# Layer 1 of a two-layer diffusion trunk: where norm 2's scale and bias are applied to its residual, and where 24 products of its modulation are computed

## The chip, the cores and the metric

The kernel runs on 1 core of one Trainium2 chip. The metric is the device time of one execution in microseconds. The engines are PE (TensorE, matrix products, with PEld for its weight loads), DVE (VectorE), ACT (ScalarE), POOL (GpSimd) and SP (SyncE, which issues nearly all the DMAs here).

## The reference, cut to what matters

Two post-norm layers over 1024 latent tokens and 256 context tokens of width 1024, all in float32. Four token mixers run side by side on one modulated stream, and a SwiGLU feed-forward follows:

```python
for l in range(2):
    m  = split(silu(c)     @ w_mod[l] + b_mod[l], 6)     # six rows of 1024
    mc = split(silu(c_ctx) @ w_mod[l] + b_mod[l], 6)
    h, hc = x * (1 + m[1]) + m[0], ctx * (1 + mc[1]) + mc[0]
    y = concat(mixers(h @ w_in[l], hc @ w_in[l])) @ w_out[l]
    x = layer_norm(alpha * x + m[2] * y, ln1_g[l], ln1_b[l])
    x = layer_norm(alpha * x + m[5] * swiglu(x * (1 + m[4]) + m[3]), ln2_g[l], ln2_b[l])
    # the same two lines for ctx with mc, in layer 0 alone
```

The change is about two things in it: the `ln2_g[0], ln2_b[0]` of the `x` that enters `alpha * x + m[2] * y` in layer 1, and the rows `m[2]`, `m[3]`, `m[4]` of layer 1.

## The kernel before, in words

**Tiles.** Tokens are cut into tiles of 128 (0 to 7 latent, 8 and 9 context). A tile of 128x1024 float32 fills one of 47 slots in SBUF that serve nearly everything. Matrix products are made from float32 operands in two parts, a high part (`hi`, cast on ACT) and the rest (`lo`, a subtraction on DVE), with three products for each pair (`split`, `mm3`). Instructions are kept in order on each engine; the order is found when the kernel is built, from the program's order and from what is expected to be ready.

**Stages.** Each layer has an in-projection (`inproj`), attention, an out-projection (`outproj`), the feed-forward's first half (`ffn_up`) and its second half (`ffn_down`, in layer 0 with `ffn_ctx` before it). In layer 1 the in-projection works through ten "c tiles" (416 columns), eight "d tiles" (512 columns, gated by a 128x128 mix) and ten "f units" (128 rows of output each).

**Modulation.** A row of `m` is made of eight products: a 128x1024 piece of `w_mod` is loaded (`mod_load`) and multiplied and summed against the broadcast `silu(c)` on DVE (`mod_tile`, L244). `silu_rows` loads that row and puts it through ACT.

**Background.** `self.bg` is a list of small steps. `background()` takes one off the list: after each tile of the in-projection, and four times in each pass of `ffn_up` over a pair of hidden blocks (19 such passes a layer, once, twice and once at three places of the pass).

**Before the change.** Layer 0's `ffn_up` has 24 modulation pieces in its background (its own row 5, layer 1's rows 1 and 0), each in two steps, a load and a product, and then 10 tiles of norm 1's scale and bias (`start`, `fetch`, `affine`). Layer 1's in-projection has 8 empty steps and then the 24 pieces of its rows 2, 4 and 3.

**The residual.** `norm2(0)` stores the normalised rows of layer 0 without scale and bias in `zd[1]`. In layer 1's `outproj`, `prepare(t)` loads such a tile (`resid_in`), multiplies it by `ln2_g` and adds `ln2_b` on POOL (`affine_row`, L1374 and L1375), and splits the tile's attention output into `ys`, four pieces on ACT (L147) and DVE (L149). `product` multiplies by the out-projection weights (L1329). `finish` gates the result (L1338), adds the residual (L1339), normalises (`stats` on DVE, `rstd` on POOL, L162 and L163, `nb` on DVE, L182) and, some tiles later, transposes pairs of tiles for the feed-forward (`to_stream`, L1255 to L1268). Tiles 0 and 1 and the last two are multiplied as pairs, the others alone; `prepare` runs one tile ahead, and at the last single tile two. Layer 0's `outproj` is the same without `affine_row`, and over ten tiles.

Of the kernel before, what the change touches and what calls it, by code (L numbers as in the profile page):

```python
# [14 lines left out]
ALU = mybir.AluOpType  # L15
# [15 lines left out]
PAUSE = 8  # L31
# [57 lines left out]
class Kern:  # L89
# [454 lines left out]
    def inproj(self, l):  # L544
        nc, a, ws = self.nc, self.a, self.ws
        last = l == DEPTH - 1
        self.cT = [self.slot(F32, "cT") for _ in range(4)]
        self.cTx = self.slot(F32, "cTx")
        base = 0 if l == 0 else self.w_in1
        def n1(t):  # L550
            return 160 if last and t >= 8 else 416
        rows = self.slot(F32, "drow")
        self.drow = rows
        self.y = [[None, None] for _ in range(4)]

        def late():
            t0 = self.slot(F32, "dws")
            nc.sync.dma_start(out=t0[:, :512], in_=a["dws"][l])
            dh, dl = self.slot(R, "dws"), self.slot(R, "dws")
            self.dws = (dh[:, :512], dl[:, :512])  # L560
            self.split(t0[:, :512], *self.dws)
            self.y[3] = [self.slot(F32, "y") for _ in range(2)]
            self.yx = [None, self.slot(F32, "yx") if not last else None]

        def load_drow():
            nc.sync.dma_start(out=rows[:, :512], in_=a["dln"][l].partition_broadcast(128))

        def load_krt():
            self.krt = self.tmp()
            nc.sync.dma_start(out=self.krt, in_=a["krt"])  # L570

        def c_tiles(units, tiles):
            self.cw = 416
            self.chunk(l, units, n1, tiles, lambda t, ps: self.post_c(l, t, ps, n1(t)))

        def d_tiles(units, tiles):
            self.cw = 512
            self.chunk(l, units, lambda t: 512, tiles, lambda t, ps: self.post_d(l, t, ps))

        def four(i):  # L580
            return [ws.get(base + i + j) for j in range(4)]

        if l == 0:
            ps, dots = self.first_stream()
            load_drow()
            load_krt()
            self.late_constants()
            late()
            units = four(4)
            for t in range(8):  # L590
                for i in POSTS.get(t, ()):
                    self.post_d(l, i, ps[i], 1)
                if t == CTX_AT:
                    for f in dots:
                        f()
                    self.first_ctx()
                c_tiles(units, [t])
            base += 4
            c_tiles(units, [8])
            ws.split_to(base + 4 + C_EARLY)  # L600
            c_tiles(units, [9])
            units = four(4)
            ws.split_to(base + 8 + F_EARLY)
            self.queue_mod(0, (2, 4, 3), (0, 1))
            d_tiles(units, (8, 9))
        else:
            self.silu_rows(("c",))
            self.queue_mod(1, (2, 4, 3), (0,), PAUSE)
            load_drow()
            load_krt()  # L610
            units = four(0)
            ws.load_to(base + 6)
            c_tiles(units, (8, 9) + tuple(range(8)))
            units = four(4)
            late()
            ws.load_to(base + 9)
            d_tiles(units, range(8))

        self.rope = [self.slot(F32, "rope") for _ in range(2)]
        for i in range(2):  # L620
            nc.sync.dma_start(out=self.rope[i], in_=a["ropeA"][i])
        self.fA = [None] * 4
        self.fB = [None] * 6
        self.fAx = self.slot(F32, "fAx")
        self.fBx = [self.slot(F32, "fBx") for _ in range(2)]
        for f in range(10):
            wh, wl = ws.get(base + 8 + f)
            ws.split_to(min(base + 10 + f, base + 18))
            ws.load_to(base + 11 + f)
            dst = self.slot(F32, "f")  # L630
            isq = f in (0, 1, 4, 5)
            for g in range(2 if last and isq else 3):
                n = 512 if g < 2 else 256
                ps = self.p1("f")
                for kt in range(8):
                    w0 = 128 * kt
                    self.mm3(
                        ps[:, :n], wh[:, w0:w0 + 128], wl[:, w0:w0 + 128], self.hT(0, kt, 512 * g, n),
                        self.hT(1, kt, 512 * g, n), kt == 0, kt == 7,
                    )  # L640
                self.tick()
                self.post_f(f, g, ps, dst)
                self.background(BG_IN)
            if f < 4:
                self.fA[f] = dst
            else:
                self.fB[f - 4] = dst
        self.flush()
        while self.bg:
            self.background()  # L650
# [636 lines left out]
    def outproj(self, l):  # L1287
        nc, a, ws = self.nc, self.a, self.ws
        last = l == DEPTH - 1
        nt = 8 if last else 10  # L1290
# [3 lines left out]
            self.affine_cols(self.sb_ff[l][c], l, c, 3, 4, self.cols[:, l, 0:8], self.cols[:, l, 8:16])  # L1294
        W = {}
        row = self.gate_row(l, 0, 2)
        if l:
            pg, pb = self.load_row(a["ln2g"][l - 1]), self.load_row(a["ln2b"][l - 1])
        self.g = [[None] * 3 for _ in range(2)]
        xs, ys, ps, zs = {}, {}, {}, []  # L1300

        def prepare(t):
            if t >= nt:
                return
            xs[t] = self.resid_in(l, t)
            if l:
                self.affine_row(xs[t], pg, pb)
            yh, yl = ys[t] = self.slot(R, "ys"), self.slot(R, "ys")
            if t < 8:
                parts = [(256 * q, 256, self.y[q][t // 4], 512, 128 * (t % 4)) for q in (3, 0, 1, 2)]  # L1310
            else:
                parts = [(512 * q, 512, self.yx[q], 256, 128 * (t - 8)) for q in (0, 1)]
            for o, n, y, w, c in parts:
                v = lambda s: s[:, o:o + n].rearrange("p (k c) -> p k c", c=128)
                self.split(y.rearrange("p (k c) -> p k c", c=w)[:, :, c:c + 128], v(yh), v(yl))
# [41 lines left out]
        for g in groups:  # L1357
# [11 lines left out]
                    ws.split_to(self.w_ff[l] + min(i // 2, 2))  # L1369
            for t in g:  # L1370
                finish(t)

    def affine_row(self, x, g, b):
        self.nc.gpsimd.tensor_tensor(out=x, in0=x, in1=g, op=ALU.mult)  # L1374
        self.nc.gpsimd.tensor_tensor(out=x, in0=x, in1=b, op=ALU.add)  # L1375


    def ffn(self, l):
# [156 lines left out]
    def ffn_up(self, l):  # L1535


        nc, ws = self.nc, self.ws
# [36 lines left out]
        for j in range(PLAIN, NHID):  # L1575
# [22 lines left out]
            self.mm12(B, W["S3"], hs["T3"], True)  # L1598
            h1 = self.tmp()
            nc.vector.tensor_tensor(out=h1, in0=A, in1=e, op=ALU.add)  # L1600
            self.background(2)
            self.mm12(X, W["g2"], hs["21"], False)
            nc.vector.tensor_tensor(out=h1, in0=B, in1=h1, op=ALU.add)
            if not last:
# [3 lines left out]
                self.mm12(pg, W["g1"], hs["x1"], True, 256)  # L1608
                self.mm12(pg, W["g2"], hs["x2"], False, 256)
            prep[3]()  # L1610
            self.mm12(A, W["S4"], hs["22"], False)
            s0 = self.tmp()
            nc.scalar.activation(out=s0, in_=X, func=AF.Silu)  # L1613
# [30 lines left out]
    def up_background(self, l):  # L1644

        nc, a = self.nc, self.a
        last = l == DEPTH - 1
        cs = (0,) if last else (0, 1)
        steps, held = [], {}

        def dots(ll, nt):
            self.mod_tile(ll, nt, held.pop("w"), cs)
            if nt % 8 == 7:
                for c in cs:
                    self.mod_finish(ll, c, nt // 8)

        def load(ll, nt):
            held["w"] = self.mod_load(ll, nt)

        for ll, v in [(l, 5)] + ([] if last else [(l + 1, 1), (l + 1, 0)]):  # L1660
            for nt in range(8 * v, 8 * v + 8):
                steps += [lambda ll=ll, nt=nt: load(ll, nt), lambda ll=ll, nt=nt: dots(ll, nt)]


        rows = []

        def start():
            rows.extend((self.load_row(a["ln1g"][l]), self.load_row(a["ln1b"][l])))
            for r in rows:
                nc.vector.tensor_scalar(out=r, in0=r, scalar1=ALPHA, scalar2=None, op0=ALU.mult)  # L1670

        def fetch(t):
            x = held["x"] = self.slot(F32, "x1")
            nc.sync.dma_start(out=x, in_=self.zd[0][128 * t:128 * t + 128])

        def affine(t):
            x = held.pop("x")
            nc.vector.tensor_tensor(out=x, in0=x, in1=rows[0], op=ALU.mult)
            nc.vector.tensor_tensor(out=x, in0=x, in1=rows[1], op=ALU.add)
            nc.sync.dma_start(out=self.zd[2][128 * t:128 * t + 128], in_=x)  # L1680

        steps.append(start)
        for t in range(8 if last else 10):
            steps += [lambda t=t: fetch(t), lambda t=t: affine(t)]
        self.silu_rows(("c",) if last else ("c", "cc"))
        return steps

    def down_blocks(self):
        out, j = [], 0
# [362 lines left out]
```

## Time and profile before

| | us |
|---|---|
| median of 3 runs | 3012.97 |
| lowest, highest | 3010.84, 3014.16 |
| the profiled execution | 3017.34 |
| its span, first to last instruction | 3015.6 |
| PE busy in the span | 2884.9 (96%) |
| DVE busy | 2125.2 (70%) |
| ACT busy | 1254.0 (42%) |
| POOL busy | 550.3 (18%) |

The profiled execution is one execution of its own; its time is 1.7 us more than its span, and 4.4 us (0.15%) above the median of the runs. Busy shares are means over stages with different limits, so a stage is read by itself.

### The profile page before, as it was taken

To read this page: it belongs to the slowest core of one execution; us is meant where nothing else is said; L and a number is where in the kernel's file an instruction comes from. 1 tells how busy PE (TensorE), PEld (TensorE's weight loads), DVE (VectorE), ACT (ScalarE), POOL (GpSimd) and SP (SyncE) were. 2 spreads that over 40 slices of the span, in tenths; PEclk is the share of its full clock that TensorE was granted. 3 is DMA by queue.
4 is the path that set the end of the run, shared out by engine and by line. 5 is a ranking of instruction groups with operands and counts; after the bars stand their busy time and mean duration, and the time that the engine had idled before them with its cause. 6 is when DMAs were issued, how large, how long until landed. Compare 5 with 4: busy or idle time off the path is not lost. (4 is left out here: it accounts for less than half of the span.)

```text
span 3015.6 us, 39143 instructions
## 1 busy us (share of the span) xinstructions
PE 2884.9 (96%) x14584; PEld 2433.9 (81%) x14584; DVE 2125.2 (70%) x3582; ACT 1254.0 (42%) x2315; POOL 550.3 (18%) x728
## 2 busy tenths in 40 slices
PE   6999989999999999999999999889998999999997
PEld 5888777878888888887887888877876888888886
DVE  8784988975666666657766562989966778557757
ACT  4534987763322222233213332987733322223211
POOL 4212554321000000000001221654442000000003
PEclk9999989999999999999999999999998999999999
DMA  6341000023133334465223240000022344226221
GB/s 245 112 148 49 7 30 8 1 87 110 50 115 115 113 112 142 152 242 183 98 81 115 75 161 28 13 31 1 15 105 77 105 154 175 84 84 230 98 70 56
DMA packets 92494, 292.43 MB, mean 97 GB/s; under 512 B 10640, under 2 KB 16400, under 8 KB 92304
## 3 DMA queue, kind: packets, MB, share of 16 engines
q1 hardware_dynamic: 92160, 289.89, 27.6%
q8 instruction: 114, 1.87, 0.3%
q14 instruction: 76, 0.62, 0.1%
q10 hardware_dynamic: 144, 0.05, 0.0%
HBM read 236.68 MB, written 53.22 MB: 96 GB/s over the span
## 5 line engine op out<-in xcount | busy, mean ns | idle before, releaser
L1827 PE MATMUL d<-whi,hid 128*128 128x512 f32 x1408 | 382.3, 391 | 6.0 <-DVE acc L1850 6.0
L149 DVE TENSOR_TENSOR wlo<-wraw,whi 128x1024 fp32r<-128x1024 f32 (+1 forms) x207 | 251.5, 1225 | 135.7 <-ACT whi L147 131.1
L1827 PEld LDWEIGHTS d<-whi,hid 128*128 128x128 f32 x1408 | 263.8, 188 | 63.0 <-DVE acc L1850 8.4
L147 ACT CAST whi<-wraw 128x1024 fp32r<-128x1024 f32 (+1 forms) x210 | 216.7, 1043 | 210.7 <-DVE wraw L1716 114.0
L162 POOL TENSOR_SCALAR v<-mv 128x1 f32<-128x1 f32 x36 | 15.6, 433 | 1576.3 <-DVE mv L173 1573.7
L1850 DVE TENSOR_TENSOR acc<-d,acc 128x1024 f32<-128x1024 f32 x129 | 156.3, 1212 | 134.5 <-PE d L1827 134.3
L777 DVE TENSOR_TENSOR PT<-pt,PT 128x512 fp32r<-128x512 f32 (+2 forms) x376 | 223.0, 609 | 25.2 <-ACT PT L776 22.4
L755 POOL TENSOR_SCALAR P<-P,r 128x640 f32<-128x640 f32 (+3 forms) x208 | 188.8, 910 | 283.8 <-DVE r L753 167.2
L773 PE MATMUL pt<-idn,P 128*128 128x128 f32 x1152 | 194.1, 281 | 28.0 <-POOL P L755 16.8
L1827 PE MATMUL d<-wlo,hid 128*128 128x512 f32 x704 | 218.9, 391 | 0.0
L776 ACT CAST PT<-pt 128x512 fp32r<-128x512 f32 (+2 forms) x376 | 191.0, 523 | 57.1 <-PE pt L773 47.7
L773 PEld LDWEIGHTS pt<-idn,P 128*128 128x128 f32 x1152 | 138.0, 142 | 66.6 <-POOL P L755 24.1
L790 PE MATMUL y<-PT,V 128*128 128x512 f32 (+3 forms) x408 | 165.4, 410 | 6.3 <-ACT PT L776 3.3
L1329 PE MATMUL o<-whi,ys 128*128 128x512 f32 x576 | 163.3, 400 | 7.5 <-DVE ys L149 5.5
L1827 PEld LDWEIGHTS d<-wlo,hid 128*128 128x128 f32 x704 | 132.4, 188 | 27.2
L791 PE MATMUL y<-PT,V 128*128 128x512 f32 (+3 forms) x408 | 149.2, 373 | 0.2 <-DVE PT L777 0.2
L1329 PEld LDWEIGHTS o<-whi,ys 128*128 128x128 f32 x576 | 109.1, 191 | 31.1 <-DVE ys L149 6.4
L244 DVE SCALAR_TENSOR_TENSOR wm<-wm,srow 128x1024 f32<-128x1024 f32 x96 | 128.3, 1348 | 2.2 <-DMA wm<-in_wmod 1.1
L1613 ACT ACTIVATE t<-X 128x512 f32<-128x512 f32 x38 | 22.8, 599 | 250.3 <-PE X L157 250.3
L155 PE MATMUL f<-h,whi 128*128 128x512 f32 x320 | 125.1, 391 | 0.0
L156 PE MATMUL f<-h,whi 128*128 128x512 f32 x320 | 124.7, 390 | 0.0
L157 PE MATMUL f<-h,wlo 128*128 128x512 f32 x320 | 124.6, 389 | 0.0
(414 smaller groups left out, 7857.4 us busy)
## 6 DMA issues: line engine op xcount, KB each, us to landing
wm<-in_wmod SPq DMA_DIRECT2D x96, 512.0 KB, 4.2
wraw<-in_wgu SPq DMA_DIRECT2D x88, 512.0 KB, 3.7
wraw<-in_wdn SPq DMA_DIRECT2D x66, 512.0 KB, 5.2
hidden<-t SPq DMA_DIRECT2D x88, 256.0 KB, 2.1
hraw<-hidden SPq DMA_DIRECT2D x44, 512.0 KB, 4.4
zd<-x SPq DMA_DIRECT2D x36, 512.0 KB, 2.7
x<-zd SPq DMA_DIRECT2D x28, 512.0 KB, 4.4
wraw<-in_wf SPq DMA_DIRECT2D x20, 512.0 KB, 3.5
```

Source lines behind the costliest of these rows:

```text
L147: a = nc.scalar.copy(hi, src)
L149: b = e.tensor_tensor(out=lo, in0=src, in1=hi.bitcast(F32), op=ALU.subtract)
L244: nc.vector.scalar_tensor_tensor(out=j, in0=w, scalar=1.0, in1=self.srow[c], op0=ALU.mult, op1=ALU.mult, accum_out=self.mod[l][c][:, nt:nt ...
L755: nc.gpsimd.tensor_scalar(out=p, in0=p, scalar1=r, scalar2=1.0, op0=ALU.mult, op1=ALU.mult)
L773: nc.tensor.transpose(tp[:, n:n + 128], p, self.idn)
L776: nc.scalar.copy(s[:, :n], tp[:, :n])
L777: nc.vector.tensor_tensor(out=s[:, 512:512 + n], in0=tp[:, :n], in1=s[:, :n].bitcast(F32), op=ALU.subtract)
L790: nc.tensor.matmul(o, v, s[:, at:at + n], start=k == 0, stop=False)
L791: nc.tensor.matmul(o, v, s[:, 512 + at:512 + at + n], start=False, stop=k == len(blocks) - 1)
L1329: nc.tensor.matmul(ps[t][:, o], x[:, c], w[:, o], start=i == 0 and n == 0, stop=i == 7 and n == 2)
L1827: nc.tensor.matmul(ps[:, o], x[:, c], w[:, o], start=n == 0, stop=n == len(todo) - 1)
L1850: nc.vector.tensor_tensor(out=acc[t][:, c], in0=ps[:, c], in1=acc[t][:, c], op=ALU.add)
```

## The change

Three edits go together.

- Layer 1's rows 2, 4 and 3 of the modulation (24 pieces) are computed in the background of layer 0's `ffn_up`, behind the 24 that were there. A piece becomes one step there: its product, and then the load of the next piece. The four background calls of a pass are spread to four places. Norm 1's scale and bias become one step per tile too: the tile's two products, its store, and the load of the next tile. Layer 1's `ffn_up` uses the same code for its own row 5 and its own eight tiles.
- Layer 1's in-projection no longer makes the `silu(c)` row nor those products. Its background has 8 empty steps, then the load of `ln2_g` and `ln2_b`, and then the eight tiles of `zd[1]`: loaded, multiplied and added to on DVE, and stored back to `zd[1]`.
- Layer 1's out-projection no longer loads the two rows, and `affine_row` on POOL is gone.

```diff
@@ inproj, layer 1
-            self.silu_rows(("c",))
-            self.queue_mod(1, (2, 4, 3), (0,), PAUSE)
             load_drow()
+            lrows = []
+            self.bg = [lambda: None] * PAUSE
+            self.bg.append(lambda: lrows.extend((self.load_row(a["ln2g"][l - 1]), self.load_row(a["ln2b"][l - 1]))))
+            self.bg += self.affine_steps(range(8), lrows, self.zd[1], self.zd[1])
@@ outproj
-        if l:
-            pg, pb = self.load_row(a["ln2g"][l - 1]), self.load_row(a["ln2b"][l - 1])
...
             xs[t] = self.resid_in(l, t)
-            if l:
-                self.affine_row(xs[t], pg, pb)
...
-    def affine_row(self, x, g, b):
-        self.nc.gpsimd.tensor_tensor(out=x, in0=x, in1=g, op=ALU.mult)
-        self.nc.gpsimd.tensor_tensor(out=x, in0=x, in1=b, op=ALU.add)
@@ ffn_up
-            self.background(2)
+            self.background()
             self.mm12(X, W["g2"], hs["21"], False)
...
             prep[3]()
+            self.background()
             self.mm12(A, W["S4"], hs["22"], False)
@@ up_background
-        for ll, v in [(l, 5)] + ([] if last else [(l + 1, 1), (l + 1, 0)]):
-            for nt in range(8 * v, 8 * v + 8):
-                steps += [lambda ll=ll, nt=nt: load(ll, nt), lambda ll=ll, nt=nt: dots(ll, nt)]
+        nts = [(l, 8 * 5 + i, cs) for i in range(8)]
+        if not last:
+            nts += [(l + 1, 8 * v + i, c) for v, c in ((1, cs), (0, cs), (2, (0,)), (4, (0,)), (3, (0,))) for i in range(8)]
...
+        steps = [lambda: load(0)] + [lambda k=k: dots(k) for k in range(len(nts))] + [start]
+        steps += self.affine_steps(range(8 if last else 10), rows, self.zd[0], self.zd[2])
...
+    def affine_steps(self, ts, rows, src, dst):
+        nc = self.nc
+        held = {}
+        def fetch(t):
+            x = held["x"] = self.slot(F32, "x1")
+            nc.sync.dma_start(out=x, in_=src[128 * t:128 * t + 128])
+        def affine(t):
+            x = held.pop("x")
+            nc.vector.tensor_tensor(out=x, in0=x, in1=rows[0], op=ALU.mult)
+            nc.vector.tensor_tensor(out=x, in0=x, in1=rows[1], op=ALU.add)
+            nc.sync.dma_start(out=dst[128 * t:128 * t + 128], in_=x)
+        def both(t, n):
+            affine(t)
+            if n is not None:
+                fetch(n)
+        return [lambda: fetch(ts[0])] + [lambda t=t, n=n: both(t, n) for t, n in zip(ts, [*ts[1:], None])]
```

(`dots(k)` now ends with `load(k + 1)`.)

## Rows read from the trace of the kernel before

**Rows 1.** The page, its first line.

```profile
span 3015.6 us, 39143 instructions
```

**Rows 2.** Stages: window, length, busy us and instructions of each engine, PEclk, DMA.

```profile
640.00:768.00 128.00, 126.46 (x602) 103.95 (x601) 74.49 (x140) 52.14 (x101) 14.26 (x32) 1.00 0.27 94
852.00:1160.00 308.00, 308.00 (x1632) 266.49 (x1631) 202.57 (x312) 72.51 (x100) 0.00 (x0) 1.00 0.36 117
2185.00:2320.00 135.00, 117.32 (x531) 94.35 (x530) 92.16 (x130) 50.17 (x94) 52.94 (x44) 0.93 0.27 99
```

**Rows 3.** Timeline of PE, layer 1's out-projection: start, us, what, [idle before <-releaser].

```profile
2196.70 1.95 PE L294 MATMUL row<-idn,mod 128*128 128x128 f32 x16
...
2209.37 2.07 PE L1329 MATMUL o<-whi,ys 128*128 128x512 f32 x4 [4.86 <-DVE ys L149]
...
2286.00 0.69 PE L1255 MATMUL th<-idn,x 128*128 128x128 f32 x2 [7.69 <-DVE t L1260]
```

**Rows 4.** Windows of 5 us there, columns as in rows 2.

```profile
2210.00:2215.00 5.00, 5.00 (x14) 3.89 (x12) 5.00 (x9) 0.00 (x0) 0.00 (x0) 0.51 0.00 0
...
2285.00:2290.00 5.00, 4.00 (x14) 3.26 (x15) 3.88 (x10) 2.69 (x6) 1.86 (x4) 0.50 0.47 187
```

**Rows 5.** The splits' line, 2199 to 2230 (layer 1), then 643 to 665 (layer 0).

```profile
L149 DVE TENSOR_TENSOR ys<-y,ys x12: 411/414/2622, 2199.7 to 2211.2; 128x256 fp32r<-128x256 f32 x12
...
L149 DVE TENSOR_TENSOR ys<-y,ys x12: 415/419/425, 643.6 to 647.7; 128x256 fp32r<-128x256 f32 x12
```

**Rows 6.** Timelines of DVE and of POOL, 2276 to 2285.

```profile
2276.80 2.32 DVE L182 SCALAR_TENSOR_TENSOR nb<-mv,v 128x1 f32<-128x1 f32 x1 [4.06 <-POOL v L163]
2279.04 5.38 DVE L149 TENSOR_TENSOR ys<-y,ys 128x256 fp32r<-128x256 f32 x3
...
2279.06 2.60 POOL L1374 TENSOR_TENSOR x<-x,lrow 128x1024 f32<-128x1024 f32 x1
```

**Rows 7.** First two tiles: layer 0 (PE, DVE), then layer 1 (DVE), timelines.

```profile
641.55 1.95 PE L294 MATMUL row<-idn,mod 128*128 128x128 f32 x16
...
664.83 2.36 DVE L1338 TENSOR_TENSOR gated<-o,row 128x1024 f32<-128x1024 f32 x2 [9.50 <-PE o L1329]
...
2229.53 2.36 DVE L1338 TENSOR_TENSOR gated<-o,row 128x1024 f32<-128x1024 f32 x2 [11.05 <-PE o L1329]
```

**Rows 8.** Lines of DVE: ns least/median/most. Products in 1711 to 1757; the residual's scale.

```profile
L244 DVE SCALAR_TENSOR_TENSOR wm<-wm,srow x8: 1192/1216/1226, 1713.6 to 1742.4; 128x1024 f32<-128x1024 f32 x8
L244 DVE DVE_READ_ACCUMULATOR wm<-wm,srow x8: 79/81/83, 1714.7 to 1743.6; 128x1 f32 x8
...
L1678 DVE TENSOR_TENSOR x<-x,lrow x18: 1214/1224/1228, 1160.6 to 2544.2; 128x1024 f32<-128x1024 f32 x18
```

**Rows 9.** One pass of `ffn_up` in layers 0 and 1; the d tiles; columns as in rows 2.

```profile
1004.34:1029.18 24.84, 24.84 (x133) 21.52 (x132) 16.25 (x24) 5.79 (x8) 0.00 (x0) 1.00 0.36 112
...
2587.14:2606.18 19.04, 19.04 (x85) 15.77 (x84) 11.43 (x16) 5.18 (x8) 0.00 (x0) 1.00 0.24 83
...
1711.00:1757.00 46.00, 46.00 (x214) 38.37 (x213) 28.04 (x63) 13.15 (x35) 11.04 (x16) 1.00 0.32 107
```

**Rows 10.** Timeline of DVE in the pass of layer 0.

```profile
1019.05 1.23 DVE L149 TENSOR_TENSOR wlo<-wraw,whi 128x1024 fp32r<-128x1024 f32 x1 [5.57 <-ACT whi L147]
```

**Rows 11.** Line L1674, the loads of norm 1's tiles: who waited; landing times.

```profile
  DVE x L1678: 9.7, 9
...
DMA to landing us min/median/max: 3.1/4.1/5.7
```

**Rows 12.** Timelines of DVE, of PE and of ACT in layer 1's in-projection.

```profile
1746.18 1.19 DVE L149 TENSOR_TENSOR wlo<-wraw,whi 128x1024 fp32r<-128x1024 f32 x1
...
1750.49 0.39 PE L157 MATMUL f<-h,wlo 128*128 128x512 f32 x1
...
1645.82 1.06 ACT L229 ACTIVATE srow<-srow 128x1024 f32<-128x1024 f32 x1
...
1648.30 0.50 PE L155 MATMUL ch<-whi,hx 128*128 128x160 f32 x1 [1.35 <-DVE t L1260]
```

More of the change, by code (lines that the diff above doesn't have):

```diff
@@ L1648, in up_background, with load, dots @@
         cs = (0,) if last else (0, 1)
-        steps, held = [], {}
-        def dots(ll, nt):
-            self.mod_tile(ll, nt, held.pop("w"), cs)
-            if nt % 8 == 7:
[L1654 to L1658, printed above, removed]
-        for ll, v in [(l, 5)] + ([] if last else [(l + 1, 1), (l + 1, 0)]):
-            for nt in range(8 * v, 8 * v + 8):
-                steps += [lambda ll=ll, nt=nt: load(ll, nt), lambda ll=ll, nt=nt: dots(ll, nt)]
-        rows = []
+        steps, held, rows = [], {}, []
+        nts = [(l, 8 * 5 + i, cs) for i in range(8)]
+        if not last:
+            nts += [(l + 1, 8 * v + i, c) for v, c in ((1, cs), (0, cs), (2, (0,)), (4, (0,)), (3, (0,))) for i in range(8)]
+        def load(k):
+            if k < len(nts):
+                held["w"] = self.mod_load(*nts[k][:2])
+        def dots(k):
+            ll, nt, c = nts[k]
+            self.mod_tile(ll, nt, held.pop("w"), c)
+            if nt % 8 == 7:
+                for i in c:
+                    self.mod_finish(ll, i, nt // 8)
+            load(k + 1)
         def start():
@@ L1670, in start @@
                 nc.vector.tensor_scalar(out=r, in0=r, scalar1=ALPHA, scalar2=None, op0=ALU.mult)
+        steps = [lambda: load(0)] + [lambda k=k: dots(k) for k in range(len(nts))] + [start]
+        steps += self.affine_steps(range(8 if last else 10), rows, self.zd[0], self.zd[2])
+        self.silu_rows(("c",) if last else ("c", "cc"))
+        return steps
+    def affine_steps(self, ts, rows, src, dst):
+        nc = self.nc
+        held = {}
         def fetch(t):
             x = held["x"] = self.slot(F32, "x1")
-            nc.sync.dma_start(out=x, in_=self.zd[0][128 * t:128 * t + 128])
+            nc.sync.dma_start(out=x, in_=src[128 * t:128 * t + 128])
         def affine(t):
@@ L1679, in affine @@
             nc.vector.tensor_tensor(out=x, in0=x, in1=rows[1], op=ALU.add)
[L1680 to L1686, printed above, removed]
+            nc.sync.dma_start(out=dst[128 * t:128 * t + 128], in_=x)
[4 more added lines that the diff above has]
+        return [lambda: fetch(ts[0])] + [lambda t=t, n=n: both(t, n) for t, n in zip(ts, [*ts[1:], None])]
     def down_blocks(self):
```

## The prediction

> **What bounds the kernel now.** I read the page first for the frame: the span is 3015.6 us [rows 1] of an execution that took 3017.34. Then the busy times stage by stage, because a mean over the kernel hides where PE waits. PE is busy without a gap through layer 0's `ffn_up`, and all but 1.5 us of the stretch that holds layer 0's out-projection; in the stretch with layer 1's out-projection it is idle for 17.7 us of 135 and its granted clock has a mean of 0.93 [rows 2]. Single passes of both layers' `ffn_up` and the d tiles of layer 1's in-projection have PE busy to the last tenth too [rows 9]. So of the four places that the change touches, three are bound by PE, and only in the fourth can work taken off other engines come back as time. The reader is to see there that POOL is busy 52.94 us against 14.26 in layer 0's counterpart.
>
> Third I read PE's timeline in that stretch for the instructions that ended its waits. Two gaps carry nearly all of it: 4.86 us at the first pair of tiles, ended by a split on DVE, and 7.69 us at the last pair, ended by DVE again [rows 3]. [...]
>
> Fourth, why DVE is late. The same twelve splits of 128x256 have a median of 0.414 and a most of 2.622 us in layer 1, and 0.419 and 0.425 in layer 0 [rows 5]. The long ones stand where POOL runs `affine_row`: at 2279.04 three splits take 5.38 us together while POOL is in one of those instructions from 2279.06 on, for 2.60; just before, DVE had waited 4.06 us for POOL's `rstd`, queued behind another of them, and a 128x1 instruction then took 2.32 [rows 6]. So POOL hurts in two ways: its queue delays the normalisation, and its run stretches DVE's instructions.
>
> **Removing `affine_row`, at the first pair.** From the gate row's first product to the first gated result layer 0 takes 664.83 - 641.55 = 23.28 us and layer 1 takes 2229.53 - 2196.70 = 32.83, for the same products [rows 3, 7]. The difference, 9.55, is the term; the gap of 4.86 and half of 5.00 us at half the clock, 2.5, are 7.4 of it, and the rest are shorter waits of the same start.
>
> **At the last pair.** The gap of 7.69 goes, if `nb` comes when layer 0's does and three splits take 1.25 instead of 5.38; half of 4.00 us at half the clock goes with it. Together 9.7 [rows 3, 4, 6]. What is late next is PE itself. The bounds of the two terms together are 12.55 (both gaps, the clock's loss stays) and 22.2 (all 17.7 us of idle time in the stretch [rows 2] and 4.5 of clock); I take 19.2, since layer 0 shows the same stage without POOL's part. The two row loads that SP no longer issues here count for nothing beside that.
>
> [...]
>
> **The row of silu(c) in layer 1.** ACT spends 1.06 us on it at 1645.82, among the casts that feed the first c tile, whose first product starts at 1648.30 after a wait of 1.35 [rows 12]. It lies in a chain of PE, ACT and DVE with no other cover, so I take all of it: 1.06, with bounds 0 and 1.35.
>
> **24 products into layer 0's `ffn_up`.** A product costs 1.216 + 0.081 = 1.30 us of DVE [rows 8]. A pass is 24.84 us of PE, and DVE is busy 16.25 of it with two pieces for two streams, 4 x 1.30 = 5.20 [rows 9]; the rest is 11.05. With four pieces a pass the first six passes have 11.05 + 8 x 1.30 = 21.45, the next six (one stream) 16.25, and the passes with four tiles of scale and bias 11.05 + 4 x 2 x 1.22 = 20.8. All are under 24.84. The cover is PE's own work, and DVE's hole of 5.57 us before the split of the next pass's first weights [rows 10] takes up the two pieces that such a pass gains, 5.2. Their loads are SP's: 24 of 512 KB, two more a pass, and behind a load stand the weights and the stores of hidden values. Should one landing a pass, 4.1 us [rows 11], be waited out in full, 21.45 + 4.1 = 25.6 exceeds the pass by 0.7; over the first six that is 4.3, the upper bound. The lower is 0, as PE has no gap to give. I take 0: in the same place the loads of norm 1's tiles made DVE wait 9.7 us over 18 tiles, 0.54 each [rows 11].
>
> **Layer 1's own `ffn_up`.** DVE needs 11.43 of 19.04 us without background [rows 9]. With four tiles in one pass it has 11.43 + 9.76 = 21.2, 2.2 more than the pass; the next has three tiles and 18.8. With 0.54 of waiting for each of four tiles the bound is 4.3. I take 0, as the backlog falls into later passes with 7.6 us free.
>
> **Eight tiles of scale and bias in the in-projection.** The tiles come at the d tiles, 46.00 us of PE in which DVE is busy 28.04 [rows 9]; eight of the 24 products leave that stretch, 10.4, and 8 x 2 x 1.22 = 19.5 come: 37.1, 8.9 idle. Waits of 0.54 each make 4.3 of that. What is queued behind a waiting `affine` on DVE are the d tiles' own norms and the split of the first f unit's weights, done at 1746.18 + 1.19 = 1747.4, which PE first reads at 1750.49: 3.1 us to spare [rows 12]. Later units are split two ahead. On SP eight stores and eight loads of 512 KB and two row loads take the place of 24 pieces and a row. Lower bound 0; upper, each landing of 4.1 waited out with nothing else in between, 17.6 + 8 x (4.1 + 2.44) - 46.0 - 3.1 = 20.8. I take 1, near the low end, where the measured waits put it. The f units lose the rest of the products, off the path, at nothing.
>
> **Sum.** -19.2 - 1.06 + 0 + 0 + 1 = -19.3 on an execution of 3017.34: 2998.0. That execution is 4.4 us above the median of the runs shown, so against the median it is 3012.97 - 19.3 = 2993.7.
>
> **Rivals.**
>
> *Part is given back* by DVE in the in-projection or in a feed-forward. For it speaks that DVE goes from 16.25 to 21.45 of 24.84, and that a tile's store and the next tile's load stand behind each other on SP. Against it are the idle times above. Price 5 to 15: 2999 to 3009. Chance 0.14.
>
> *Only one of the two gaps goes*: the last pair's splits follow on each other's heels on ACT and DVE also without POOL. For it speaks that `prepare` makes two tiles in one step there; against it that layer 0, with a context pair at its end, has no such gap [rows 2]. Gain 9.55 + 1.06 - 1 = 9.6: 3003.4. Chance 0.06.
>
> *The change does not do what it says*: the splits were slow for some other reason (ACT, or loads at the stage's start), PE waits as before: 3012. Rows 5 and 6 speak against it. Chance 0.04.
>
> *Slower: DVE waits at each tile in the d stage.* The mechanism is an `affine` at the head of DVE's queue before its tile has landed, so that the f units' weights are split late. With the longest landing, 5.7, at every tile [rows 11] the stall is 17.6 + 8 x (5.7 + 2.44) - 46.0 - 3.1 = 33.6, and PE's clock costs 2.5 more: 3012.97 - 20.3 + 36.1 = 3028.8. PE begins to wait from 1.5 us a tile on, the gain is gone at 3.7, and over 0.2% is lost from 4.5 on. Against it speaks 0.54. Chance 0.04.
>
> **How the numbers follow.** The forecast, all but a microsecond or two of the term kept, has 0.72 and 2991 to 2998 by itself. About 0.2%, 6 us, is what a measurement of this kernel can tell from no change. Faster by more: 0.72 + 0.06 and 0.12 of the first rival, 0.90. Within it: the 0.04 of no effect and 0.02 of the first rival, 0.06. Slower: 0.04. The range goes from 2990 (the upper bounds of the gains, 22.2 + 1.35) to 3004, which takes in the second rival and half of the first; what it leaves out is about 0.16.
>
> **What would show it.** In layer 1's out-projection: POOL under 15 us, every split near 0.42, no gap of PE over 1.5 us, granted clock 1.00 from the first tile to the last, first pair done 23.3 us after the gate row. In layer 0's `ffn_up` the pass stays 24.84 and DVE rises to some 21.5 in the first six; a longer pass there is the wrong step. In the in-projection the first f unit follows the last d tile without a gap; a wait for `wlo` there is the slower rival at work. The prediction is wrong as a whole if a gap of several microseconds, ended by DVE, is still in the out-projection.

## The result, and the profile after

| | us |
|---|---|
| before, median of 4 runs | 3012.93 |
| after, median of 4 runs (2983.80 to 2996.27) | 2986.75 |
| ratio, with its 95% interval | 0.9917 [0.9906, 0.9929] |
| the profiled execution after, and its span | 2988.27, 2986.1 |
| PE, DVE, ACT, POOL busy in the span | 2868.1, 2114.7, 1253.2, 509.6 |

The change makes the kernel 26.2 us faster, 6.9 more than the forecast's 19.3, and 3.3 us below the low end of its range. POOL is busy 40.7 us less than before. DVE took over its sixteen instructions and is still busy less than before, 2114.7 against 2125.2.

To find where the time came from, the span of each profiled execution was cut where the first or the last product of a stage starts on PE. "To c" goes from layer 0's last down-projection product to the first c tile, "c, d" and "f" are the tiles of layer 1's in-projection, "out 1" runs from layer 1's gate row to its last out-projection product.

| us | attention 0 | ffn_up 0 | to c | c, d | f | attention 1 | out 1 | ffn_up 1 |
|---|---|---|---|---|---|---|---|---|
| before | 356.7 | 471.9 | 6.1 | 101.7 | 131.9 | 314.8 | 112.8 | 363.6 |
| after | 351.3 | 472.0 | 4.9 | 99.7 | 132.9 | 313.0 | 93.5 | 363.6 |

The other stages differ by 0.4 at most. Layer 0's attention lies ahead of all that the change touches, with the same instructions in the same order in both kernels, and over the twelve other executions that were profiled (the experiments below) it took 351.1 to 359.0 us; its 5.4 is left out of the account here and comes back at its end.

**Layer 1's out-projection.** Window of the kernel before, from the gate row to the last product, columns as in [rows 2]:

```profile
2196.70:2309.50 112.80, 98.18 (x433) 79.78 (x432) 74.55 (x99) 35.89 (x69) 41.66 (x33) 0.94 0.21 75
```

Windows of the kernel after: the same stretch; in layer 0's `ffn_up` the 308 us that answer to those of [rows 2], and one pass for that of [rows 9].

```profile
2186.91:2280.40 93.49, 92.99 (x432) 76.70 (x431) 53.79 (x99) 35.68 (x69) 9.38 (x20) 1.00 0.24 88
...
846.40:1154.40 308.00, 308.00 (x1632) 266.58 (x1631) 225.91 (x364) 73.88 (x101) 0.00 (x0) 1.00 0.49 156
...
998.74:1023.58 24.84, 24.84 (x134) 21.52 (x133) 21.14 (x37) 5.76 (x8) 0.00 (x0) 1.00 0.58 178
```

In the out-projection PE is idle for 0.5 us of 93.49, against 14.6 of 112.80, and its granted clock is 1.00 throughout. DVE's busy time there falls by 20.8 us, more than the sixteen instructions cost elsewhere (16 x 1.22 = 19.5). Layer 0's `ffn_up` takes the products without PE noticing: the pass is still 24.84, with DVE at 21.14 instead of 16.25.

The splits' line of the kernel after, 2175 to 2212, then the start of the gate row on PE and of the first gated result on DVE (timelines):

```profile
L149 DVE TENSOR_TENSOR ys<-y,ys x12: 418/419/425, 2188.9 to 2193.1; 128x256 fp32r<-128x256 f32 x12
```

```profile
2186.91 1.95 PE L294 MATMUL row<-idn,mod 128*128 128x128 f32 x16
```

```profile
2210.13 2.36 DVE L1337 TENSOR_TENSOR gated<-o,row 128x1024 f32<-128x1024 f32 x2 [9.49 <-PE o L1328]
```

No split is stretched: the most is 425 ns, against 2622 in [rows 5]. The first pair takes 2210.13 - 2186.91 = 23.22 us, against 32.83 before and layer 0's 23.28 [rows 7].

**Layer 1's in-projection.** PE's timeline around the first c tile and at the first f unit, and then DVE's just before that:

```profile
1637.82 0.66 PE L1258 MATMUL th<-idn,acc 128*128 128x128 f32 x4 [1.02 <-ACT acc L183]
1639.39 1.99 PE L1258 MATMUL th<-idn,acc 128*128 128x128 f32 x8 [0.91 <-DVE t L1263]
1641.25 0.50 PE L155 MATMUL ch<-whi,hx 128*128 128x160 f32 x1
...
1742.81 0.50 PE L157 MATMUL f<-h,wlo 128*128 128x512 f32 x1 [0.75 <-DVE wlo L149]
```

```profile
1738.94 1.22 DVE L1684 TENSOR_TENSOR x<-x,lrow 128x1024 f32<-128x1024 f32 x1
...
1740.41 1.22 DVE L1685 TENSOR_TENSOR x<-x,lrow 128x1024 f32<-128x1024 f32 x1
1741.54 1.22 DVE L149 TENSOR_TENSOR wlo<-wraw,whi 128x1024 fp32r<-128x1024 f32 x1
```

Of three waits ahead of the first c tile the third, 1.35 us [rows 12], is gone with the row of `silu(c)`. At the first f unit a wait of 0.75 has come: its split on DVE stands behind the last tile's scale and bias.

Windows from the first c tile to the first f unit, of the kernel before and then of the kernel after:

```profile
1648.30:1750.04 101.74, 100.22 (x485) 89.92 (x485) 54.66 (x151) 36.08 (x106) 24.22 (x51) 0.92 0.31 110
...
1641.25:1740.98 99.73, 98.19 (x485) 87.98 (x485) 59.27 (x147) 36.17 (x106) 25.18 (x52) 0.94 0.39 136
```

PE is idle for 1.5 us in both, so the 2.0 us between them are its granted clock. The full clock does not come back with the third wait: in the kernel after, its mean there is 0.94, against 0.92.

### The profile page after: what moved, and what is told of

Read it like the earlier page. It is cut to its first block, busy times and chain, and to the rows that moved or that the text cites. A ratio compares the mean times of both kernels' runs of the same rounds, so it can differ in the third digit from the quotient of the medians.

```text
span 2986.1 us, 39167 instructions
## 1 busy us (share of the span) xinstructions
PE 2868.1 (96%) x14584; PEld 2418.1 (81%) x14584; DVE 2114.7 (71%) x3598; ACT 1253.2 (42%) x2314; POOL 509.6 (17%) x712
## 5 line engine op out<-in xcount | busy, mean ns | idle before, releaser
L780 DVE TENSOR_TENSOR PT<-pt,PT 128x512 fp32r<-128x512 f32 (+2 forms) x376 | 223.1, 610 | 22.0 <-ACT PT L779 19.3
L155 PE MATMUL B<-T,whi 128*128 128x512 f32 x304 | 118.5, 390 | 0.0
```

Of the source, the lines that this page charges most:

```text
L155: mm(ps, lh, rh, start=first, stop=False, skip_group_check=more)
L780: nc.vector.tensor_tensor(out=s[:, 512:512 + n], in0=tp[:, :n], in1=s[:, :n].bitcast(F32), op=ALU.subtract)
```

## Experiments

Each time is a median and stands beside runs of the kernel before on the same chip (their medians 3012.53 to 3013.24). The stages of the profiled executions are in one table at the end of this section.

**1. The changed kernel once more**, unedited, for its scatter.

> The changed kernel once more, to tell what in the two profiles is the change and what is one execution's own. Between the profiles the out-projection of layer 1 (gate row to the last product) went from 112.8 to 93.5 us, 19.3 less; the start of layer 1's in-projection lost 1.6 and its c and d tiles 2.0; the f units gained 1.0; layer 0's attention, whose instructions stand in the same order in both kernels, was 5.3 shorter and layer 1's 1.8. Theory A: the change is worth the first four, 21.9, a ratio of 0.9927; the attention stages scatter by some 5 us from execution to execution whatever the kernel, with the granted clock. Then layer 0's attention (285.1 to 636.2 here) lasts anything from 351 to 357 in this profile, and the out-projection again 93.5. Theory B: the attention of layer 0 is faster for good, and the change is worth 27 to 29, a ratio near 0.990; then that stage is again within 1 us of 351.

2987.63 us (2981.64 to 2997.89 over 6 runs), ratio 0.9917 [0.9903, 0.9932]. The gain repeats, and so does the scatter: ten runs of one program spread over 16 us. In this profile layer 0's attention took 357.4 us instead of 351.3 and the c and d tiles 102.8 instead of 99.7, as theory A allows; its ratio of 0.9927 lies inside the interval and theory B's 0.990 just outside. The forecast's -19.3 is a ratio of 0.9936, outside both intervals.

**2. The out-projection's part alone**: before without `affine_row` and its two row loads. Layer 1's residual then lacks norm 2's scale and bias.

```diff
-        if l:
-            pg, pb = self.load_row(a["ln2g"][l - 1]), self.load_row(a["ln2b"][l - 1])
...
-            if l:
-                self.affine_row(xs[t], pg, pb)
```

> The kernel before, without the two POOL instructions for each tile and the two row loads: the scale and bias of layer 0's norm 2 are left out of layer 1's residual, nothing else differs. Theory A: all of the out-projection's gain and nothing else, 19.3: 2993.6, the stage at 93.5, first pair done 23.3 after the gate row. The rival (the splits were late for another reason, the loads at the stage's start or ACT): the two gaps of 4.86 and 7.69 stay, no gain. If the gain is 26 as in the changed kernel, everything measured comes from here and the rest of the change is worth nothing.

2996.26 us, 0.9939 [0.9926, 0.9952]: 17.0 us less, and the interval holds the 19.3 expected. "Out 1" falls to 93.5, as after the whole change, and no other stage that the change touches moves.

**3. The products alone**: after, with the residual back on POOL in the out-projection (`nc.gpsimd` for both instructions, in `prepare` as before).

> The change without its residual part: the 24 products go into layer 0's feed-forward, the four places are spread, and the residual stays on POOL in the out-projection. Theory A: the out-projection as before (112.8, both gaps), the in-projection's start 1.6 and its tiles up to 2.0 shorter since ACT no longer makes the row of silu(c), no wait at the first f unit; 3009 to 3011. Theory B (the products in the in-projection cost more than the profile shows): 3006 or less.

3006.30 us, 0.9978 [0.9968, 0.9988]. With "out 1" at 111.5, the third wait ahead of the c tiles is gone and those tiles take 95.8. So moving the products, with the row, gains 6.6 us by this ratio (3.6 to 9.6 by its interval), where the forecast had 1.06. The time lies at the border of theory B.

**4. The residual alone**: before, with the eight tiles on DVE in the in-projection, behind the 24 products that stay there.

```diff
             self.queue_mod(1, (2, 4, 3), (0,), PAUSE)
+            lrows = []
+            self.bg.append(lambda: lrows.extend((self.load_row(a["ln2g"][l - 1]), self.load_row(a["ln2b"][l - 1]))))
+            self.bg += self.affine_steps(range(8), lrows, self.zd[1], self.zd[1])
             load_drow()
...
-            if l:
-                self.affine_row(xs[t], pg, pb)
```

> The change without its products: they stay in layer 1's in-projection with the row of silu(c), and the scale and bias of the residual come behind them on DVE, during the f units. Theory A: the out-projection at 93.5, the in-projection's start as before, no new wait of the f units over 1 us as DVE is busy 16 of 67 us in the last of them: a gain of 19.3, 2993.6. Rival: DVE's longer list delays the f units' splits or the start of attention, and 2 to 6 of it are given back.

2997.29 us, 0.9945 [0.9933, 0.9957]: equal to experiment 2 within the intervals, and "f" stays 131.9. So the sixteen DVE instructions cost nothing that shows when they come during the f units.

**5. DVE in POOL's place**: after, with the two instructions on DVE in the out-projection's `prepare`.

```diff
...
-            self.bg += self.affine_steps(range(8), lrows, self.zd[1], self.zd[1])
...
+            if l:
+                self.nc.vector.tensor_tensor(out=xs[t], in0=xs[t], in1=pg, op=ALU.mult)
+                self.nc.vector.tensor_tensor(out=xs[t], in0=xs[t], in1=pb, op=ALU.add)
```

> The changed kernel, but the residual's scale and bias stay in the out-projection, on DVE instead of POOL: the engine is changed and the place is not. By the theory that POOL's instructions held up DVE's splits, the long splits (2.6 us) vanish; DVE has 2.44 more for each tile of 10.9 us and is under 60% busy there, but at the first pair the four tiles' 9.8 us stand among twelve splits and six weight splits of the start, so the out-projection comes to 94 to 98 us and the time to within 5 us of the changed kernel, 2988 to 2993. By the rival, that it is the place (work at the out-projection's start) and not the engine, the first gap of some 5 us stays, with the clock's loss: 101 us or more there.

2994.53 us, 0.9938 [0.9926, 0.995]; "out 1" is 103.5. DVE's timeline at the first pair, and PE's one long wait:

```profile
2194.59 1.22 DVE L1306 TENSOR_TENSOR x<-x,lrow 128x1024 f32<-128x1024 f32 x1
2195.72 0.42 DVE L149 TENSOR_TENSOR ys<-y,ys 128x256 fp32r<-128x256 f32 x1
2196.06 1.22 DVE L1307 TENSOR_TENSOR x<-x,lrow 128x1024 f32<-128x1024 f32 x1
2197.20 2.35 DVE L1306 TENSOR_TENSOR x<-x,lrow 128x1024 f32<-128x1024 f32 x2
2199.47 2.35 DVE L1307 TENSOR_TENSOR x<-x,lrow 128x1024 f32<-128x1024 f32 x2
2201.74 1.09 DVE L149 TENSOR_TENSOR ys<-y,ys 128x256 fp32r<-128x256 f32 x3
2202.74 3.48 DVE L149 TENSOR_TENSOR wlo<-wraw,whi 128x1024 fp32r<-128x1024 f32 x3
```

```profile
2204.01 1.22 PE L1329 MATMUL o<-wlo,ys 128*128 128x512 f32 x2 [5.48 <-DVE wlo L149]
```

No split is stretched, but six of the instructions stand in front of the weights' splits, and PE waits 5.48 us. The stage is the rival's, which said 101 or more. So the engine is not all of the gain.

**6. POOL in DVE's place**: after, with the two instructions on POOL in the in-projection (`affine_steps(..., nc.gpsimd)`).

> The changed kernel, with the two instructions of each of the eight tiles on POOL again, but left in the in-projection. Theory (the place decides: in the out-projection nothing covers DVE, in the in-projection PE does): the out-projection stays at 93.5 us from the gate row to the last product, DVE's splits in the d stage are stretched to some 2.6 us without a wait of PE, and the time is that of the changed kernel, 2984 to 2991. Rival (the engine decides, POOL hurts wherever it runs beside DVE): PE waits in the d stage or the f stage, c and d tiles together above 105 us or f units above 135, and the time is 2995 or more.

3001.35 us, 0.9968 [0.9956, 0.998]. "Out 1" stays 93.5, but "f" is 142.2: the rival. Timelines of DVE, of POOL, and of PE:

```profile
1733.05 2.07 DVE L149 TENSOR_TENSOR dvl<-t,dvh 128x256 fp32r<-128x256 f32 x1 [0.47 <-ACT dvh L147]
...
1747.92 2.55 DVE L484 SCALAR_TENSOR_TENSOR t<-t,v,drow 128x256 f32<-128x256 f32 x1 [4.40 <-POOL v L163]
1750.39 1.21 DVE L149 TENSOR_TENSOR wlo<-wraw,whi 128x1024 fp32r<-128x1024 f32 x1
```

```profile
1732.37 2.46 POOL L1686 TENSOR_TENSOR x<-x,lrow 128x1024 f32<-128x1024 f32 x1
...
1744.64 2.34 POOL L1685 TENSOR_TENSOR x<-x,lrow 128x1024 f32<-128x1024 f32 x1 [3.83 <-DMA x<-zd]
1747.06 0.19 POOL L162 TENSOR_SCALAR v<-mvd 128x1 f32<-128x1 f32 x1
```

```profile
1743.31 0.79 PE L155 MATMUL f<-h,whi 128*128 128x512 f32 x1 [3.73 <-ACT whi L147]
...
1751.66 0.79 PE L157 MATMUL f<-h,wlo 128*128 128x512 f32 x1 [7.13 <-DVE wlo L149]
```

PE's cover holds while DVE's splits are stretched to 2.07 beside POOL. The wait of 3.73 comes from POOL's queue: a norm's `v` stands behind POOL's instructions, DVE waits 3.19 us for it and ACT for DVE, and ACT's cast of the f unit's weights stands behind that. The longer wait comes where POOL waits 3.83 us for a late tile: the norm's `v` is queued behind it, DVE waits 4.40 for `v`, the f unit's split is queued behind DVE's wait, and PE waits 7.13. That is the slower rival of the prediction, on another engine.

The kernel before has the same chain at its second gap. POOL's timeline there:

```profile
2273.46 2.40 POOL L1374 TENSOR_TENSOR x<-x,lrow 128x1024 f32<-128x1024 f32 x1 [6.68 <-DMA x<-zd]
```

POOL had waited 6.68 us for that tile, and the `rstd` for which DVE then waited 4.06 [rows 6] was queued behind it. The prediction named POOL's queue and missed that a late load stood at its head.

Experiments 3, 5, 6 and the changed kernel make a square of POOL or DVE, in the out-projection or ahead: 3006.3, 2994.5, 3001.4 and about 2987. From the first of them the engine alone gains 11.8 us, the place alone 5.0, and both 19.3. The 5.0 is not clear of noise (0.9968 [0.9956, 0.998] against 0.9978 [0.9968, 0.9988]); by stages the place alone takes 18.0 us off "out 1" and adds 10.3 to "f" and 4.9 to "c, d".

**7. The row of silu(c) back** in layer 1's in-projection, unread: after, with one line more.

```diff
         else:
+            self.silu_rows(("c",))
             load_drow()
```

> The changed kernel with the row of silu(c) made again at the head of layer 1's in-projection, though nothing reads it: a load and 1.06 us of ACT. In the profiles with that row (before, no scale, residual only) the stretch from the last down product to the first c tile is 6.0 to 6.1 us and the c and d tiles are 101.7 to 101.8, with the clock at 0.50 for over ten microseconds from the first c tile on; without the row (changed twice, products only) they are 4.6 to 4.9, and 95.8, 99.7 and 102.8. Theory A: the row's 1.06 us make a third wait of PE of 1.35, after which the clock always falls. Then it is 6.1 and 101.7 again, and the time 2 to 5 us longer than the changed kernel's: 2990 to 2993. Theory B: the loads of the products on SP are what made the c tiles slower; then the row alone costs 1.3 at most and the c and d tiles stay scattered.

2991.85 us (2991.39 to 2997.42), 0.9932 [0.992, 0.9943]: 5.1 us above the changed kernel's first median, 4.2 above its second. Timeline of PE and windows of 5 us, columns as in [rows 2]:

```profile
1638.78 0.66 PE L1259 MATMUL th<-idn,acc 128*128 128x128 f32 x4 [1.02 <-ACT acc L183]
1640.35 1.74 PE L1259 MATMUL th<-idn,acc 128*128 128x128 f32 x8 [0.91 <-DVE t L1264]
1643.45 0.50 PE L155 MATMUL ch<-whi,hx 128*128 128x160 f32 x1 [1.35 <-DVE t L1264]
```

```profile
1645.00:1650.00 5.00, 5.00 (x26) 5.00 (x25) 0.22 (x1) 2.26 (x4) 0.42 (x3) 0.50 0.79 291
1650.00:1655.00 5.00, 5.00 (x23) 4.95 (x23) 0.45 (x2) 0.37 (x2) 0.89 (x3) 0.50 0.80 296
```

The third wait is back, and behind it PE's granted clock is 0.50 for more than ten microseconds. The times are theory A's, but two limits hold. The interval overlaps the changed kernel's [0.9906, 0.9929], so the row's price is not clear of noise. And the clock falls without the row too: in the kernel after, in experiment 1 and in experiments 5, 8 and 11 it is at 0.50 from the first c tile on; only in 3 and 6 does it hold there, to fall for some microseconds later in the c tiles (0.66 in one window of 5 us in 3, 0.75 and 0.91 in two in 6).

**8. Two empty steps instead of eight** (`[lambda: None] * 2`), so that the tiles come earlier.

> The changed kernel with 2 empty steps instead of 8 ahead of the residual's tiles, so that they come at the c tiles, where DVE is idle 22 of 49 us, and no longer in front of the first f unit's split. Theory: the wait of 0.75 at the first f unit and the 1.0 of the f stage go (131.9 again); nothing else changes: 1 us less than the changed kernel. Rival: at the c tiles they stand in the way of the c tiles' norms or their loads in the way of the weights, and the stage gets longer by 1 to 4.

2994.99 us (2986.94 to 3001.25), 0.9937 [0.9922, 0.9953]. The f units are back at 131.9, but the c and d tiles take 105.3. SP's timeline, and PE's wait:

```profile
1689.97 10.33 SPq L1686 DMA_DIRECT2D zd<-x  x4
1700.35 1.24 SPq L62 DMA_DIRECT2D wraw<-in_wc  x2
```

```profile
1701.24 0.50 PE L156 MATMUL ch<-wlo,h 128*128 128x512 f32 x1 [1.80 <-DVE wlo L149]
```

The tiles' stores stand in front of weight loads on SP. The empty steps keep them behind the c tiles' weights. This is the rival, at the cost of 1.9 us more idle time of PE in the c and d tiles; most of the rest is a mean clock of 0.91 there, as in experiment 1 with its 102.8.

**9. PE kept busy ahead of the c tiles**: after, with four unread 128x512 products behind layer 0's last down-projection.

```diff
+                if ends and not last and t == 7:
+                    wp = self.p2("wp")
+                    for _ in range(4):
+                        nc.tensor.matmul(wp[:, :512], self.hid[js[-1]][0][:, :128], self.wdn[js[-1]][0][:, :512], start=True, stop=True)
```

> The changed kernel with four products of 512 columns more on PE, into a buffer that nothing reads, behind the last down product of layer 0, where PE waits 1.02 us for the norm of the last tiles. Theory A (the scatter of the c and d tiles is the clock, which falls or does not fall at this place): with one of the two waits filled, the clock is 1.00 at the first c tile in this profile, the c and d tiles last 95 to 97 us, and the median is 2 to 4 us below the changed kernel's, with less scatter. Theory B: the scatter has another cause; nothing changes, or the four products cost their 0.9 us.

2984.99 us (2981.21 to 2988.53), 0.9908 [0.9894, 0.9923]. They fill the first wait of 1.02. Windows at the c tiles:

```profile
1640.00:1645.00 5.00, 4.95 (x38) 4.04 (x38) 4.26 (x12) 4.42 (x9) 2.17 (x6) 1.00 0.65 234
1645.00:1650.00 5.00, 5.00 (x36) 4.97 (x36) 1.06 (x5) 1.86 (x5) 2.21 (x7) 1.00 0.73 252
```

The granted clock is 1.00 through all the c and d tiles, which take 94.2 us. That is what they cost without a loss of clock, 7.5 less than before the change, and experiment 10 repeats it. It is theory A.

**10 and 11. Seventeen empty steps instead of eight**, with the four products (10) and without (11).

> The kernel with four unread products on PE behind layer 0's feed-forward, and 17 empty steps instead of 8, so that the residual's tiles come at the last d tile and the ten f units. Theory (the first f unit's wait for its weights, 0.75 us, comes from the tiles' instructions on DVE in front of its split): the wait is gone, the f units take 131.9 us instead of 133.0, the c and d tiles stay near 94.2, and the time is some 1 us below the kernel with the four products alone, near 2984. Rival (the tiles disturb wherever they stand): a wait of about as much comes at a later f unit or at the start of attention, and the time is equal or up to 5 us more.

> The changed kernel with 17 empty steps instead of 8, without the four products. Theory: the f units take 131.9 us instead of 132.9, and the time is that of the changed kernel less 1 us, 2986 with its scatter of some 8 us either way from the clock ahead of the first c tile. Rival (the tiles disturb wherever they stand): equal or up to 5 us more.

2986.17 us, 0.9917 [0.9903, 0.9932], and 2989.59, 0.9925 [0.991, 0.9939]. The wait at the first f unit is gone, but "f" falls only to 132.3 and 132.5; neither time differs from its kernel with eight steps, so neither theory is shown.

**12. The same four products in the kernel before**, which still makes the row of `silu(c)`.

> The kernel before, with the same four unread products on PE behind layer 0's feed-forward; the row of silu(c) stays in the in-projection. Theory (the clock falls when the waits ahead of the first c tile come one behind the other, the row's 1.35 as the third): with the first wait of 1.02 filled, 0.91 and 1.35 remain, so the clock falls less often or not at all; 0 to 7.5 us less than before, 3005 to 3013, and if the clock stays at 1.00 the c and d tiles take 95 instead of 101.7. Rival (the last wait alone decides): the clock falls as before, c and d tiles 101 to 102, and the time is within 1 us of before.

3014.07 us, 1.0007 [0.9998, 1.0016]: no gain, and the theory of the succession of waits fell. Timeline of PE and a window:

```profile
1645.54 1.75 PE L1255 MATMUL th<-idn,acc 128*128 128x128 f32 x8 [0.91 <-DVE t L1260]
1648.64 0.47 PE L155 MATMUL ch<-whi,hx 128*128 128x160 f32 x1 [1.36 <-DVE t L1260]
```

```profile
1650.00:1655.00 5.00, 5.00 (x25) 5.00 (x25) 0.41 (x3) 2.45 (x4) 0.41 (x3) 0.50 0.82 285
```

The first wait is filled, the last of 1.36 remains, and the clock falls as before. So with the row's wait in place the clock is lost even without the first one. That this wait alone decides is not shown, since the kernel after loses the clock without it.

Stages of the profiled executions, as in the table above, read to about 0.1 us:

| us | to c | c, d | f | attention 1 | out 1 |
|---|---|---|---|---|---|
| 1, again | 4.8 | 102.8 | 132.9 | 313.1 | 93.6 |
| 2, neither scale nor bias | 6.1 | 101.7 | 131.9 | 314.7 | 93.5 |
| 3, products only | 4.6 | 95.8 | 131.9 | 313.8 | 111.5 |
| 4, residual only | 6.0 | 101.8 | 131.9 | 315.1 | 93.6 |
| 5, DVE in place | 4.8 | 102.8 | 131.9 | 313.5 | 103.5 |
| 6, POOL ahead | 4.7 | 100.7 | 142.2 | 313.1 | 93.5 |
| 7, row back | 6.0 | 101.6 | 132.9 | 312.9 | 93.6 |
| 8, two steps | 4.8 | 105.3 | 131.9 | 314.5 | 93.6 |
| 9, PE busy | 4.7 | 94.2 | 133.0 | 311.6 | 93.5 |
| 10, busy, 17 steps | 4.6 | 94.2 | 132.3 | 314.9 | 93.5 |
| 11, 17 steps | 4.8 | 99.7 | 132.5 | 313.0 | 93.5 |
| 12, before, PE busy | 6.0 | 101.8 | 131.9 | 314.8 | 112.9 |

## Why the prediction was right in the out-projection and wrong in its time

**The out-projection: right, to a tenth.** The first pair gained 32.83 - 23.22 = 9.6 (forecast 9.55), the rest of the stage 19.3 - 9.6 = 9.7 (forecast 9.7). Of the 19.3, 14.1 is idle time, 14.6 less 0.5, and 5.2 is PE's busy time, 98.18 less 92.99, whose mean granted clock was 0.94 and is 1.00. The two gaps named were 12.55 of the 17.7 us of idle time in the prediction's stretch, less than its "nearly all"; the gaps with their clock, granted at 0.51 and 0.50 behind them [rows 4], come to 4.86 + 2.5 + 9.7 = 17.1, 2.2 short, and taking layer 0's stage as the measure was the better choice. That it came out to a tenth is luck: the same stage with POOL took 111.5 us in experiment 3, 1.3 less than before. Experiment 6 shows the stretching itself in another stage: of the d tiles' eight splits the four beside a POOL instruction took 2.03 to 2.07 us and the four others 0.41 to 0.43.

**Layer 0's `ffn_up` and layer 1's: right at 0.** The passes keep 24.84 us, DVE has 21.14 where 21.45 was worked out, and both stages keep their 472 and 364 us.

**Eight tiles in the in-projection: right at 1, in part by luck.** The f units take 1.0 us more, with a wait of 0.75 for the first `wlo`. The forecast's 1 stood for waits for tiles, and DVE waited for none of the eight; the 3.1 us to spare was used up by DVE's work in front of the split, so this wait is not the slower rival's. Experiments 5 and 8, without those instructions there, have 131.9.

**The row of silu(c) and the products leaving the in-projection: the step that failed.** The forecast had "I take all of it: 1.06, with bounds 0 and 1.35" for the row, and "off the path, at nothing" for the products. Experiment 3, which has this part alone, gained 6.6 us (3.6 to 9.6). The wait itself was sized rightly: "to c" loses 1.2. But the upper bound left out the clock behind the wait, though the same prediction counted half the clock behind the gaps of the out-projection. PE's idle time in the c and d tiles is 1.5 us before, after and in experiments 3, 9 and 12 alike; what moves them between 94.2 and 102.8 us is the granted clock.

How much of the miss is the row alone is open. In all five profiled executions with the row (before, 2, 4, 7 and 12) the c and d tiles take 101.6 to 101.8 us, 7.5 above the 94.2 of full clock. Without it and without the four products of experiments 9 and 10 they take 95.8 (experiment 3), 99.7 (the kernel after, 11) and 102.8 (1, 5): less in the mean, but not always. On the runs' medians the row costs 4.2 to 5.1 us (experiment 7), not clear of noise. Moving the products while the row stays gains 4.8 in the medians (experiment 7's gain of 20.8 less experiment 4's of 16.0), again not clear of noise, where the forecast had 0. With the row left in, the forecast would be 19.2 - 1 = 18.2, a ratio of 0.9940, and experiment 7's interval of 0.992 to 0.9943 holds it.

**The range.** With 4.7 for the row, the middle of the two, the sum is 19.2 + 4.7 - 1 = 22.9 and the time 2990.1. The other 3.3 us to the measured median are no more than half the width of the ratio's interval (0.00115 x 3013 = 3.5). They stay open. Two places could hold them, both stages whose granted clock differs. Layer 1's attention took 314.7 to 315.1 us in the four profiled executions with the products left in the in-projection (before, 2, 4 and 12) and 311.6 to 314.9 in the ten others. Layer 0's attention took 356.6 to 359.0 us in those four (mean 357.4) and 351.1 to 357.4 in the ten others (mean 352.9), with the same instructions; its granted clock is 0.91 and 1.00 in the first such stretch that differs (280 to 300 us, before and after). But there the chip may count for more than the change: on the chip of experiments 1 to 4 it took 356.0 to 359.0, with the products moved (1, 3) or not (2, 4), and on that of 5, 7, 8 and 9 351.1 to 352.5. One profile of each kernel doesn't settle it. The range's low end, 2990, was made of the terms' upper bounds alone (3012.97 - 22.2 - 1.35 = 2989.4), without the scatter that a kernel has whose clock falls for longer in some executions than in others: of the changed kernel's ten runs the two longest, 2996.27 and 2997.89 us, have a mean granted clock of 0.984 and 0.985, the shortest, 2981.64, 0.993.

**The rivals.** Nothing of size was given back and both gaps went. The slower rival did not occur on DVE, whose tiles were there in time, but experiments 6 and 8 show that it was near: POOL's queue, with one late tile at its head, made "f" 10 us longer, and six empty steps fewer cost some 8 in the medians.

**A better version?** The kernel of experiment 9 has the lowest median, 2984.99, but its interval overlaps that of the changed kernel; a gain over it isn't shown.

## What to carry to other kernels

Price a short wait of PE by what the clock does behind it as well: here a dense stage took 94.2 us at full clock and 99.7 to 102.8 where the clock fell behind waits of 0.9 to 1.35 us ahead of it. When work leaves an engine that stretches its neighbour (here POOL, beside which splits of 0.42 us took up to 2.62), ask both which engine takes it and under what cover: here the engine alone gave 11.8 of 19.3 us, and the place alone 5.0, which is not clear of noise. A kernel's other layer, with the same stage and without the suspect, was here a better measure of the gain (19.2 for 19.3) than the sum of the gaps (17.1).

## What the runs showed of the hardware

- The same program loses PE's full clock for longer in one execution than in another. With waits of 1.0 and 0.91 ahead of them, the c and d tiles of the changed kernel took 99.7 us in one execution (mean granted clock 0.94) and 102.8 in the other (0.91), and 95.8 in experiment 3 (0.98), whose waits there are 0.96 and 0.91. With a wait of 1.35 as the last one they took 101.6 to 101.8 every time (0.92), whether the first wait was there or not. With the 0.9 alone (experiments 9 and 10) they took 94.2 twice (1.00). What sets the length in one execution is not shown.
- A 128x1024 instruction with two inputs took 2.36 to 3.46 us on POOL (median 2.40 for the product and for the sum, the kernel before) and 1.19 to 1.23 on DVE (the kernel after).
